# Giving the last two heads of one middle store, and of the last one, to the first four DMA engines

## The chip, the cores and the metric

One core of a Trainium2 chip. The metric is the device time of one execution in microseconds (us). A program on one core is compared by several executions of both kernels on the same chip.

## The reference, cut to what matters

```python
batch, seq, heads, dim = 16, 512, 16, 64
q_rot = rope(q, cos, sin); k_rot = rope(k, cos, sin)       # rotate halves of dim
scores = np.einsum('bshd,bthd->bsht', q_rot, k_rot)        # float32, 16 x 512 x 16 x 512
```

The result has 268 MB, the inputs 67 MB. Four fifths of what moves are stores of scores.

## The kernel before

The work goes in 64 steps (`NST = B * C`). A step makes the scores of 128 rows for all 16 heads: eight pairs of matmuls into PSUM, eight ScalarE copies into a stage tile of 128 x 16 x 512 floats (32 KB a row), one store of 4 MB from SP's queue. There are three stage tiles.

```python
stage_pool = ctx.enter_context(tc.tile_pool(name="stage", bufs=3))
...
def store(i, st):
    o = o_v[i // C, i % C]
    if i < NST - 1:
        nc.sync.dma_start(o, st)          # 128 rows: all 16 engines, 8 rows each
        return
    h = H - 2
    nc.sync.dma_start(o[:, :h], st[:, :h])
    nc.sync.dma_start(o[:116, h:], st[:116, h:])   # 116 rows: 4 engines, 29 rows each
    nc.sync.dma_start(o[116:, h:], st[116:, h:])   # 12 rows: 12 engines, one row each
...
for i in range(C, NST):
    ...                                    # transposes, rope on VectorE, scores(), store(i, st)
    if i % C == C - 2:
        load("q", i // C + 2)              # after steps 6, 10, ... 30, 34, ...
    elif i % C == C - 1:
        load("k", i // C + 3)              # after steps 7, 11, ... 31, 35, ...
```

The last store already hands most of its last two heads to four DMA engines.

## Time and profile before

| | before |
|---|---|
| median of 3 runs | 800.3 us (800.18 to 802.09) |
| profiled span | 799.0 us |
| busiest compute engine | PE, 87% |
| transfers of SP's queue | 98.6% of 16 engines' time |
| mean rate | 421 GB/s |

How to read it: DMA is at its limit, the compute engines are not. But a share of 98.6% over sixteen engines does not tell whether all of them are the limit. For that the packets have to be followed one by one, which the prediction does. It calls the engine that ends last X. The lines themselves are in the prediction.

### The profile page before, as it was taken

The page shows a single profiled execution, that of the slowest core. Times are in us where ns is not written, and L with a number is a line of the kernel's source. Part 1 is how long each engine was busy: PE and PEld are TensorE (multiplying, and loading weights), DVE is VectorE, ACT ScalarE, POOL GpSimd, SP SyncE. Part 2 cuts the span into 40 slices and gives each one's busy share as a digit, 9 for nine tenths or more (in the row PEclk, how much of TensorE's full clock was granted, in tenths as well). Part 3 has the DMA queues.
Part 4 walks back from the last instruction along what each step waited for, and adds up shares of the span by engine and source line. Part 5 has one row for each costly group of instructions (what it writes and reads, how often), then busy time and mean ns, then how long its engine had stood idle before and what let it go on. Part 6 is the DMA issues. An engine that isn't in the chain of part 4 may idle for free.

```text
span 799.0 us, 7715 instructions
## 1 busy us (share of the span) xinstructions
PE 691.3 (87%) x3072; PEld 299.3 (37%) x3072; DVE 544.6 (68%) x516; ACT 561.2 (70%) x647; POOL 0.7 (0%) x6
## 2 busy tenths in 40 slices
PE   4989998997979979799797997979979799799970
PEld 2444443343434334343343443424434343344420
DVE  6999987676866768577585775857758478585300
ACT  3888886775857758577585775757757677578870
POOL 0000000000000000000000000000000000000000
PEclk9999999898998989889898898988989899899995
DMA  9999999999999999999999999999999999998995
GB/s 355 422 424 424 432 427 433 425 435 427 421 437 426 439 427 430 433 431 430 431 428 433 434 428 429 433 438 420 418 426 434 435 415 418 426 440 375 422 439 231
DMA packets 17844, 336.17 MB, mean 421 GB/s; under 512 B 1808, under 2 KB 3088, under 8 KB 4240
## 3 DMA queue, kind: packets, MB, share of 16 engines
q1 hardware_dynamic: 17520, 335.55, 98.6%
q8 instruction: 24, 0.39, 0.2%
q10 hardware_dynamic: 288, 0.13, 0.1%
q14 instruction: 12, 0.10, 0.0%
HBM read 67.24 MB, written 268.44 MB: 420 GB/s over the span
## 4 chain that ended last, share of the span: by engine, by line
DMA 50%; PE 40%; ACT 4%; DVE 3%; issue 1%; ACTq 0%; SPq 0%; DVEq 0%
DMA out_dram<-st 47%; PE ps L166 30%; PE bank L127 10%; ACT st L173 4%; DMA q_sb<-in_q_dram 2%; DVE part L106 1%; DMA early<-in_k_dram 1%; DVE q_sb L107 0%; DVE k_sb L107 0%; DVE k_sb L111 0%; DVE q_sb L111 0%; DVE early L107 0%; DVE kT_t L142 0%; ACTq L281 0%; DVE early L111 0%
## 5 line engine op out<-in xcount | busy, mean ns | idle before, releaser
L173 ACT COPY st<-ps 128x1024 f32<-128x1024 f32 x512 | 494.7, 1018 | 203.7 <-DMA out_dram<-st 105.6
L166 PE MATMUL ps<-kT_t,qT_t 64*128 64x512 f32 x2048 | 548.9, 654 | 71.0 <-ACT st L173 70.9
L166 PEld LDWEIGHTS ps<-kT_t,qT_t 64*128 64x128 f32 x2048 | 185.0, 197 | 261.7 <-issue 144.6
L142 DVE COPY qT_t<-bank 128x512 f32<-128x512 f32 x118 | 81.6, 691 | 203.8 <-PE bank L127 203.8
L127 PEld LDWEIGHTS bank<-ident,q_sb 128*128 128x128 f32 x480 | 55.6, 152 | 102.5 <-issue 99.1
L127 PE MATMUL bank<-ident,q_sb 128*128 128x128 f32 x480 | 86.9, 308 | 0.9 <-PE ps L166 0.9
L127 PEld LDWEIGHTS bank<-ident,k_sb 128*128 128x128 f32 x480 | 50.5, 141 | 95.4 <-issue 38.7
L127 PE MATMUL bank<-ident,k_sb 128*128 128x128 f32 x480 | 78.7, 287 | 1.6 <-DVE qT_t L142 1.2
L142 ACT COPY kT_t<-bank 128x512 f32<-128x512 f32 x122 | 72.5, 599 | 6.4 <-PE bank L127 6.4
L107 DVE TENSOR_TENSOR q_sb<-q_sb,cos_t 128x1024 f32<-128x1024 f32 x60 | 73.5, 1226 | 2.1
L111 DVE TENSOR_TENSOR k_sb<-k_sb,part 128x1024 f32<-128x1024 f32 x60 | 73.5, 1225 | 2.1
L107 DVE TENSOR_TENSOR k_sb<-k_sb,cos_t 128x1024 f32<-128x1024 f32 x60 | 73.5, 1225 | 2.0
L106 DVE TENSOR_TENSOR part<-q_sb,ss_t 128x1024 f32<-128x1024 f32 x60 | 73.5, 1225 | 2.0
L106 DVE TENSOR_TENSOR part<-k_sb,ss_t 128x1024 f32<-128x1024 f32 x60 | 73.0, 1216 | 0.1
L111 DVE TENSOR_TENSOR q_sb<-q_sb,part 128x1024 f32<-128x1024 f32 x60 | 73.0, 1216 | 0.0
L127 PE MATMUL bank<-ident,early 128*128 128x128 f32 x64 | 10.5, 316 | 12.5 <-DVE early L111 10.6
L127 PEld LDWEIGHTS bank<-ident,early 128*128 128x128 f32 x64 | 8.3, 161 | 17.5 <-issue 13.4
L106 DVE TENSOR_TENSOR part<-early,ss_t 128x1024 f32<-128x1024 f32 x8 | 9.8, 1223 | 5.9 <-DMA early<-in_k_dram 5.8
L111 DVE TENSOR_TENSOR early<-early,part 128x512 f32<-128x512 f32 x16 | 10.3, 687 | 0.2
L107 DVE TENSOR_TENSOR early<-early,cos_t 128x1024 f32<-128x1024 f32 x8 | 9.8, 1225 | 0.3
L142 ACT COPY qT_t<-bank 128x512 f32<-128x512 f32 x10 | 5.7, 617 | 3.2 <-PE bank L127 3.2
L142 DVE COPY kT_t<-bank 128x512 f32<-128x512 f32 x6 | 4.1, 685 | 0.3 <-PE bank L127 0.3
(9 smaller groups left out, 2.8 us busy)
## 6 DMA issues: line engine op xcount, KB each, us to landing
out_dram<-st SPq DMA_DIRECT2D x59, 4096.0 KB, 23.9
k_sb<-in_k_dram SPq DMA_DIRECT2D x15, 2048.0 KB, 26.9
q_sb<-in_q_dram SPq DMA_DIRECT2D x15, 2048.0 KB, 29.9
out_dram<-st SPq DMA_DIRECT2D x16, 1024.0 KB, 14.3
out_dram<-st SPq DMA_DIRECT2D x1, 3584.0 KB, 20.4
early<-in_k_dram SPq DMA_DIRECT2D x1, 1536.0 KB, 8.9
early<-in_q_dram SPq DMA_DIRECT2D x1, 1536.0 KB, 12.1
early<-in_k_dram SPq DMA_DIRECT2D x1, 512.0 KB
```

The lines of the kernel that those rows point to most:

```text
L106: nc.vector.tensor_tensor(pv, xs, ss, op=mult)
L107: nc.vector.tensor_tensor(xc, xc, cs, op=mult)
L111: nc.vector.tensor_tensor(y, y, z, op=add)
L127: nc.tensor.transpose(bank[:, x, :], src, ident)
L142: copy(out=dst, in_=src)
L166: nc.tensor.matmul(out=po, lhsT=lhs[64 * r : 64 * r + 64, :], rhs=rh, start=True, stop=True)
L173: nc.scalar.copy(out=so, in_=si)
```

## The change

The intent is to take bytes from the engines that end late and give them to the four lowest-numbered ones, once at step 30 and more completely in the last store. Transfers of 116 and of 4 rows run on engines 0 to 3 only, as the prediction derives.

```diff
+    UNEVEN = (30, NST - 1)
...
-        if i < NST - 1:
+        if i not in UNEVEN:
             nc.sync.dma_start(o, st)
             return
         h = H - 2
         nc.sync.dma_start(o[:, :h], st[:, :h])
-        nc.sync.dma_start(o[:116, h:], st[:116, h:])
-        nc.sync.dma_start(o[116:, h:], st[116:, h:])
+        for rows in (slice(0, 116), slice(116, 120), slice(120, 124), slice(124, P)):
+            nc.sync.dma_start(o[rows, h:], st[rows, h:])
```

## The prediction

> **What bounds the kernel now.** I read the page first, top down. It has one row that is full and none among the engines.
>
> ```profile
> span 799.0 us, 7715 instructions
> PE 691.3 (87%) x3072; PEld 299.3 (37%) x3072; DVE 544.6 (68%) x516; ACT 561.2 (70%) x647; POOL 0.7 (0%) x6
> DMA  9999999999999999999999999999999999998995
> q1 hardware_dynamic: 17520, 335.55, 98.6%
> ```
>
> The four compute engines stop short of 90%. The transfers of SP's queue fill 98.6% of what sixteen DMA engines can give in 799.0 us, at a mean of 421 GB/s. So the transfers are the bound, and the open question is whether all sixteen engines are, or one of them. The second view was busy time by stretch, at the end of the run (columns: stretch in us, its length, the engines, granted clock, DMA share, GB/s):
>
> ```profile
> 750.00:777.00 27.00, 23.71 (x100) 9.45 (x100) 3.83 (x5) 21.38 (x23) 0.00 (x0) 0.94 0.99 426
> 777.00:789.00 12.00, 0.20 (x2) 0.00 (x0) 0.00 (x0) 1.32 (x2) 0.00 (x0) 0.73 0.96 408
> 789.00:795.00 6.00, 0.00 (x0) 0.00 (x0) 0.00 (x0) 0.00 (x0) 0.00 (x0) 0.50 0.30 107
> 795.00:799.00 4.00, 0.00 (x0) 0.00 (x0) 0.00 (x0) 0.00 (x0) 0.00 (x0) 0.50 0.04 15
> ```
>
> Here the reader sees that sixteen engines do not end together. From 789 to 795 a mean share of 0.30 is about five of sixteen; after 795 at most one works. Who is it? The trace keeps a record of every DMA packet (queue, start, duration, bytes), not its engine. But on a busy engine the next packet starts 3 to 4 ns before the last one's recorded end, and each engine must work through the same list (8 packets of 32,768 B for a whole store, then one of 4 B for the semaphore). So I followed the packet that ended last (797.64 us) backwards. The chain goes back to 25 us through 935 packets with one gap over 20 ns (329 ns at 745 us, under an instruction fetch). This one engine, which I call X, never rests. Its 32,768-byte store packets have a median of 1.246 us, against 1.213 us over all engines; its 16,384-byte load packets are not slow (0.61 us). X is late by what its stores lose: in the semaphore landings of each store, the sixteenth comes 1.0 us after the fifteenth at 40 us, 3.3 us after it at 437 us and 6.9 us after it at 797.8 us. X is the bound; the other fifteen have slack.
>
> Does X ever wait for the kernel? Each store was issued between 8.2 and 17.4 us before X took its first packet (from store 4 on), so X always has work queued. The third view, the waits, agrees:
>
> ```profile
> ACT st L173 <- DMA out_dram<-st: 105.6, 28, 6.0
> SPq L147 <- ACT st L173: 657.0, 59, 16.6
> ```
>
> ScalarE waits 105.6 us for a free stage buffer, that is for X's last packet of an old store. The chain of waits is the same told in time: a store's flight, then some 20 us of matmuls, then the next.
>
> ```profile
> 408.91 28.12 DMA out_dram<-st
> 437.04 0.04 ACTq L173
> 437.08 0.04 issue
> 437.12 1.02 ACT st L173
> ```
>
> Only the DMA in this chain is X's time; the matmuls run while X works off its backlog.
>
> **What the Trainium skill says.** "DMA: Bandwidth & Descriptors", section "Why a DMA increments its semaphore by 16 and not by 1": a transfer runs on the largest k up to 16 that divides its slowest dimension on both sides, on the lowest-numbered k engines. Then 128 rows give 16 engines, 116 rows give 4 (29 rows each), 12 rows give 12, 4 rows give 4. The trace agrees in number: SP issues 112 transfers, and there are 1776 four-byte packets = 110 x 16 + 4 + 12. X did exactly one 4,096-byte packet at the end, after its 28,672-byte ones, so X is among engines 4 to 11, not among the first four. The same page, "Latency and other measured facts", calls engines 7 and 15 usually slower than the rest; X could be 7, but no record here gives the number. The same page, "Anatomy of one DMA — SWDGE (gpsimd) path", says that DMA engines do not wait on semaphores, only the issuing sequencer does; X's gapless chain agrees.
>
> **The change, part by part.** The store of step 30 (issued at 381.89 us, on X from 396.87 to 406.88) loses its last two heads, 4 KB of 32 KB in each row; these 128 rows go out in transfers of 116 + 4 + 4 + 4 rows, all on engines 0 to 3.
>
> - X, step 30. Before: eight packets, 1.251 us from one start to the next, plus the semaphore, 10.017 us. After: eight of 28,672 B. At the same rate each takes 0.875 x 1.251 = 1.095 us (an estimate; when compute had ended, the trace shows 1.062 us for that size against 1.213 for 32,768, the same ratio). Saved: 8 x 0.156 = 1.25 us.
> - X, last store. Its one row of the 12-row transfer goes to engines 0 to 3: 0.165 us saved (797.471 to 797.636), directly on the end.
> - Engines 0 to 3, step 30. Instead of eight packets of 1.213 us (9.7 us) they get eight of about 1.06 and 32 of 4,096 B. Those took 0.159 us at the median and 0.200 at the mean in the last store: 8.5 + 32 x 0.2 = 14.9 us, 5.2 us more each. Beside X.
> - Engines 0 to 3, last store. Two rows more than their 30, about 0.3 to 0.4 us each. They ended at 794.06 to 794.79, X at 797.64. With X at 797.64 - 1.25 - 0.17 = 796.2, and the others' start also earlier, as it hangs on stage buffers which X frees, they still end about 2 us before it.
> - SP. Four more issues at step 30, two more at the end. The present ones of this kind took:
>
> ```profile
> 778.35 0.70 SPq L152 DMA_DIRECT2D out_dram<-st  x1
> 779.10 1.19 SPq L153 DMA_DIRECT2D out_dram<-st  x1
> ```
>
> Some 3 to 4.5 us of SP's time (an estimate from these two), which delays the q load issued next. At step 30 that load waits 23.7 us in X's queue before its first packet, so this is hidden.
> - Buffers. A stage tile is free when all of its transfers have landed, now five. On engines 0 to 3 this can be later than on X: relative to X they lose 5.2 + 1.25 = 6.4 us, and the fifteenth landing was about 2.7 us ahead of X near 400 us. In the worst case (one of the four is that fifteenth) step 33 may start filling its tile 3.7 us after X is done instead of at once. X's backlog at the following stores is 11.7 us or more, so even that does not empty X's queue.
>
> Sum: -1.25 - 0.17 = -1.42 us, less up to 0.1 for the crowding described below: -1.4. The time becomes 800.3 - 1.4 = 798.9 us, the profiled span 797.6.
>
> **The rivals.**
> - Nothing is gained at step 30, because the 4 KB rows, though moved by other engines, are still read from X's part of the memory and hold X up by as much. For it: X's rate is near what any engine reaches (27.0 GB/s), and in the last store 4,096-byte packets stretched from 0.159 up to 0.5 us. Against it: in that last store engines 0 to 3 read all 116 rows, X's eight among them, while X wrote its eight 28,672-byte packets. These took 1.062 us five times, otherwise 1.080, 1.146 and 1.189. The two in the time of the crowd lost 0.1 us together; the small packets gave way. This rival would make 800.1 us.
> - The four engines become the bound: their extra 5.2 us holds back the buffer, the next stores come late, X runs dry. For it: ScalarE's waits end with a store's last landing, and only three stage tiles exist. Against it: the backlog of 11.7 us. It would make up to 802 us if X lost what the worst case above costs (3.7 us, less the 1.4 gained).
> - The middle part is absorbed: the kernel waits elsewhere later, so what X saves at 400 us is idle time by 740 us. For it: PE is at 87% and busy 29.38 of the 30 us from 720 to 750. Against it: X has no gap after 25 us but the one fetch, and its backlog at the end is still 8 to 11 us. Only the last store's 0.17 us would remain: 800.1 us.
>
> **Range and chances.** All outcomes lie within 0.4% of 800.3. I put some 75% on the main line (798.9), 20% on the two rivals without gain (800.1) and 5% on a loss. Runs of the kernel before scatter from 800.18 to 802.09, which adds more to the upper end than the lower. Range 798.0 to 800.2. Faster by over 2% would need 16 us, ten times what X sheds; slower by as much needs X starved for the same time. Within 2%: 0.985.
>
> **What would show it right or wrong.** In the packets of X, step 30's store should be eight of about 1.095 us in place of 1.25, with the chain still free of gaps; every later landing of X should be about 1.25 us earlier than before, and the issues of the last stores too. After the last 28,672-byte packet X should have nothing, and the trace should end about 1.4 us earlier, still with X. Rival one shows as step-30 packets on X that stay near 1.25 us; rival two as gaps in X's chain after 420 us, or a later last landing of the store of step 30 that delays the issues after it for good; rival three as a gap in X's chain between 410 and 790 us. The prediction is wrong as a whole if the last packet belongs to an engine of the first four, or if the time does not fall by 0.5 us at least.

## The result, and the profile after

| | before | after |
|---|---|---|
| median of 6 runs | 800.85 us (799.82 to 802.09) | 801.0 us (799.6 to 802.69) |
| ratio after / before | | 1.0001, 95% interval 0.9984 to 1.0017 |
| profiled span | 799.0 us | 799.7 us |

A ratio here is the mean time of one kernel's fast runs over that of the other's of the same rounds, so not quite the ratio of the medians. The time did not move. The prediction of 798.9 us, 1.4 us under before, was wrong, and the measured 801.0 lies outside its range of 798.0 to 800.2.

The page after, its first lines:

```profile
span 799.7 us, 7724 instructions
PE 682.3 (85%) x3072; PEld 295.5 (37%) x3072; DVE 544.6 (68%) x516; ACT 561.3 (70%) x647; POOL 0.7 (0%) x6
DMA  9999999999999999999999999999999999998996
q1 hardware_dynamic: 17664, 335.55, 98.5%
```

The bound is the same. The queue has 144 packets more: at step 30, 128 rows make two packets each instead of one, and four transfers on four engines add 4 x 4 packets of 4 B. The 4 x 4 agree with the rule of the largest divisor that the prediction cites. (In the last store 4 + 12 semaphore packets became 4 x 4, the same sum, which shows nothing.)

The end of the run, busy time by stretch after the change (columns as in the prediction):

```profile
750.00:777.00 27.00, 23.28 (x108) 9.31 (x104) 3.90 (x5) 22.04 (x24) 0.00 (x0) 1.00 1.00 426
777.00:789.00 12.00, 0.00 (x0) 0.00 (x0) 0.00 (x0) 0.52 (x1) 0.00 (x0) 0.63 1.00 430
789.00:795.00 6.00, 0.00 (x0) 0.00 (x0) 0.00 (x0) 0.00 (x0) 0.00 (x0) 0.50 0.35 119
795.00:799.70 4.70, 0.00 (x0) 0.00 (x0) 0.00 (x0) 0.00 (x0) 0.00 (x0) 0.50 0.11 38
```

After 795 us the DMA share is 0.11 where it was 0.04: besides X, some of the four favoured engines are now still at work. Their last packet ended at 797.48 us, X's at 798.26 (797.64 before). So X is still the last, but by 0.8 us only.

The waits and the chain after the change:

```profile
ACT st L174 <- DMA out_dram<-st: 122.7, 40, 6.2
SPq L148 <- ACT st L174: 631.6, 57, 16.6
```

```profile
407.15 30.25 DMA out_dram<-st
437.40 0.02 issue
437.43 0.04 ACTq L174
437.46 0.04 issue
437.50 1.02 ACT st L174
```

ScalarE waits 122.7 us for stage tiles instead of 105.6, yet X's chain of packets has no gap after step 30 but one under an instruction fetch. X was not starved; what the other engines wait for costs nothing.

SP's issues around step 30, first before, then after (start, duration in us, engine, line, operation, count):

```profile
381.89 0.33 SPq L147 DMA_DIRECT2D out_dram<-st  x1
382.32 0.89 SPq L79 DMA_DIRECT2D q_sb<-in_q_dram  x1
```

```profile
382.09 0.33 SPq L152 DMA_DIRECT2D out_dram<-st  x1
383.73 3.42 SPq L154 DMA_DIRECT2D out_dram<-st  x4
387.26 0.89 SPq L80 DMA_DIRECT2D q_sb<-in_q_dram  x1
```

The four pieces took 3.42 us of SP, as estimated, and the q load was issued 5 us later. It still lay 18.5 us in X's queue, so the delay itself was hidden.

Now X's packets at step 30. No view of the profile prints single packets; these were read from the trace file and followed as the prediction describes. Before: eight of 1.25 us, the store and the q load behind it together 14.89 us. After: 1.121, 1.095, 1.086, 1.091, 1.095, 1.114 and 1.105 us, close to the 1.10 that was predicted, and then an eighth of 1.581; the first packet of the q load took 1.406 us instead of 0.611. Store and load together: 14.94 us. X had saved 1.25 us and had lost it again within 3 us of time. That is the finding which the experiments had to explain.

Busy time by stretch for 404 to 408 us, before and then after, points the same way:

```profile
404.00:408.00 4.00, 4.00 (x22) 1.83 (x20) 3.90 (x4) 3.76 (x6) 0.00 (x0) 1.00 0.99 414
```

```profile
404.00:408.00 4.00, 4.00 (x21) 1.79 (x20) 3.67 (x3) 3.74 (x5) 0.00 (x0) 1.00 1.00 364
```

The engines are as busy as before (0.99 and 1.00), but move 364 GB/s in place of 414. They are not idle; their packets take longer. But this stretch alone proves little: later runs that lose the same have 375 to 413 GB/s in it (e1, e3, e13), and e6, which loses nothing, has 387. The reading rests on the packets.

### The profile page after: what moved, and what is told of

Its sections match the earlier page's. It is cut to its first block, busy times and chain, and to the rows that moved or that the text cites. A ratio compares the mean times of both kernels' runs of the same rounds, so it can differ in the third digit from the quotient of the medians.

```text
span 799.7 us, 7724 instructions
## 1 busy us (share of the span) xinstructions
PE 682.3 (85%) x3072; PEld 295.5 (37%) x3072; DVE 544.6 (68%) x516; ACT 561.3 (70%) x647; POOL 0.7 (0%) x6
## 4 chain that ended last, share of the span: by engine, by line
DMA 50%; PE 36%; DVE 5%; ACT 5%; issue 1%; ACTq 0%; DVEq 0%
DMA out_dram<-st 50%; PE ps L167 27%; PE bank L128 9%; ACT st L174 5%; DVE part L107 2%; DVE early L112 1%; DVE k_sb L112 1%; DVE k_sb L108 1%; DVE early L108 1%; DMA early<-in_k_dram 1%; DVE kT_t L143 0%; DVE q_sb L108 0%; DVE q_sb L112 0%; ACTq L282 0%; DVE qT_t L143 0%
## 5 line engine op out<-in xcount | busy, mean ns | idle before, releaser
L174 ACT COPY st<-ps 128x1024 f32<-128x1024 f32 x512 | 494.8, 1019 | 203.3 <-DMA out_dram<-st 122.7
L167 PE MATMUL ps<-kT_t,qT_t 64*128 64x512 f32 x2048 | 540.0, 644 | 79.2 <-ACT st L174 79.2
L167 PEld LDWEIGHTS ps<-kT_t,qT_t 64*128 64x128 f32 x2048 | 181.3, 194 | 265.4 <-issue 134.6
```

The costliest lines, as they stand in the source:

```text
L167: nc.tensor.matmul(out=po, lhsT=lhs[64 * r : 64 * r + 64, :], rhs=rh, start=True, stop=True)
L174: nc.scalar.copy(out=so, in_=si)
```

## The experiments

Two measures are used throughout. "Store plus load" is X's time from the first packet of step 30's store to the end of the q load behind it: 14.89 us before, 13.64 us if the 1.25 us are kept. "Excess" of a load is what its 128 packets of 16 KB take over their undisturbed 0.611 us, in sum over all sixteen engines.

The edits below are abridged; words stand for the lists of slices. My first theory, **A**, was chance: a 16 KB instruction fetch is recorded at 406.3 us, and such fetches ride on the DMA engines. The rival, **B**: what X sheds comes back to it by a cause of the change. Four runs on one chip came first.

### e1: the middle part alone

```diff
-        for rows in (four pieces):
+        for rows in ((slice(0, 116), slice(116, P)) if i == NST - 1 else (four pieces)):
```

> Only the store of step 30 is split; the last store is that of the kernel before. Theory A (the slow DMA engine X really sheds about 1.25 us at step 30; the profile after hid it under an instruction fetch of 1.28 us that fell on X by chance, and the last store cost X 0.4 us more than before instead of 0.17 us less): 1.2 us faster than before on average, ratio 0.9985; in the trace X's packets of step 30 take about 1.10 us in place of 1.25, and X's end is 796.4 us plus 1.3 us for each 16 KB instruction fetch and 0.6 us for each 8 KB one that falls on X. Theory B (what X sheds comes back to it, as slower packets or as a wait): ratio 1.000, X's outliers in the microseconds after step 30 in this run too, without a fetch there.

Measured: 800.1 us against 800.44, ratio 1.0000 (0.9987 to 1.0013). X's step-30 packets were seven of 1.09 to 1.11 us and an eighth of 1.453; store plus load 15.21 us. Theory A's 0.9985 is outside the interval, and the loss is there again.

### e2: steps 20 and 40 in place of 30, last store of before

```diff
-    UNEVEN = (30, NST - 1)
+    UNEVEN = (20, 40, NST - 1)
```

(The last store is that of before here and in all that follow, unless told.)

> Two middle stores split, steps 20 and 40; the last store is that of the kernel before. Theory A: twice 1.25 us, 2.5 us faster, ratio 0.9969. Theory B: ratio 1.000. A third reading, the first four engines become the bound when they are given 128 rows of 4 KB twice (about 4.2 us more each time): the last packets belong to them, after 796 us, and the gain is under 1 us.

Measured: 808.76 us, ratio 1.0084 (1.0055 to 1.0112). The six runs fall into two groups, 803.0 and 803.3, and 807.9 to 810.0; what parts them was not looked for. I had thought of the third reading, but not of its size. The end of the run by stretch:

```profile
789.00:795.00 6.00, 0.00 (x0) 0.00 (x0) 0.00 (x0) 0.00 (x0) 0.00 (x0) 0.50 0.52 216
795.00:799.00 4.00, 0.00 (x0) 0.00 (x0) 0.00 (x0) 0.00 (x0) 0.00 (x0) 0.50 0.24 85
799.00:805.00 6.00, 0.00 (x0) 0.00 (x0) 0.00 (x0) 0.00 (x0) 0.00 (x0) 0.50 0.14 54
```

From 795 to 799 a share of 0.24 is four engines of sixteen. The last packet of all, a small one of one of the first four engines, ended at 804.7 us, X's own share at 796.1. One of the four, followed back, took 13.69 us for step 20 and 14.78 for step 40 in place of 9.69: 9.1 us more in all. That used up their slack and more. So engines 0 to 3 cannot take a second middle split of this size.

### e3: the changed kernel again

No edit.

> The changed kernel once more, unaltered. Theory A: on average some 0.8 us faster than before (1.25 at step 30, less 0.4 in the last store), ratio 0.999, and another draw of the fetches that fall on X: step 30 or the load after it no longer has the 1.28 us in this trace unless a fetch record overlaps it. Theory B: ratio 1.000, and X slowed by about 1.3 us at step 30 and the load behind it again.

Measured: 800.71 us against 800.44, ratio 0.9998 (0.9986 to 1.001). X's eighth packet 1.214 us, the load's first packet 1.116, store plus load 14.33 us. A 16 KB fetch leaves a different mark on the engine it falls on: in e1, at 274 us, on an engine other than X, 0.91 us without any packet and then a packet that took 0.50 us longer. On X at step 30 there is no such hole: the next packet starts 6 ns after the last. In e3 the long packets also began at 405.4 us, two microseconds before the next fetch record (407.4). **Theory A fell**: the loss is in all three traces that have the split at step 30, and it is not a fetch.

### e4: which engine is X?

```diff
+        for rows in pieces of 68, 4, 5, 6, 7, 8, 9, 10 and 11 rows:      # last store only
```

> The kernel before with its last two heads of the last store cut in pieces of 68, 4, 5, 6, 7, 8, 9, 10 and 11 rows, so that by the rule of the largest divisor they run on the lowest 4, 4, 5, 6, 7, 8, 9, 10 and 11 engines, one row on each (17 for the 68). The number of 4096-byte packets that the slow engine X does after its 28672-byte ones tells its number: 7 for engine 4, 6 for 5, 5 for 6, 4 for 7, 3 for 8, 2 for 9, 1 for 10, 0 for 11 and more. I expect 4, engine 7. The time is not the point (the last pieces wait for earlier landings): 798 to 803 us.

Measured: one run, 806.52 us (the last pieces waited for semaphores). I first counted four small packets on X and took it for engine 7. That count was wrong: it crossed a pause of 1.4 us and went on with another engine's packets. In the unbroken stretch right behind X's last 28 KB packet (from 801.32 to 802.13 us) there are five, each with its semaphore packet. They must be those of 5, 6, 7, 8 and 9 rows: those of 10 and 11 rows would run on the idle lower engines at the same time, and between 801.32 and 802.45 us no other engine starts a small packet. Only engine 4 gets all five without being one of the first four. **X is engine 4.** I saw this only after e8.

### e5, e6, e7: what disturbs the load?

In e1, e3 and the changed kernel the q load behind step 30 had an excess of 8.8, 9.5 and 10.2 us; before it had 1.9. So X is not alone: in the changed kernel 23 of that load's 128 packets took over 0.64 us, up to nine of them at the same moment; in the kernel before 9 did, up to four at a time. Several engines are slowed. Theory **C** put this down to engines 0 to 3 being late against the rest; theory **D** to small packets or extra issues next to a load.

e5 sends the last two heads of step 30 in four pieces of 32 rows, on all sixteen engines:

```diff
+        for rows in (slice(0, 32), slice(32, 64), slice(64, 96), slice(96, P)):   # i == 30
```

> Step 30 is split as in the change, but its last two heads go out in four pieces of 32 rows, which run on all 16 engines, two rows each; last store as before. In the three runs with the change's step 30 engine X (number 7) saved about 1.25 us in the store and lost 0.7 to 1.6 us in that store's last packet and the first packets of the q load behind it, and the 128 packets of that q load took 8.8 to 10.2 us more than their undisturbed 611 ns in sum over all engines, against 1.9 in the kernel before. Theory C (the loss comes from putting engines 0 to 3 late against the rest): no excess here, the load's sum under 4 us, X's store plus load 14.9 to 15.1 us as before (the same bytes in smaller packets). Theory D (the loss comes from the five issues or the 4 KB packets in front of the load): the sum again 8 us or more and X's store plus load 15.5 us or more.

Measured: one run, 801.01 us. The excess of the load was 7.9 us and X's store plus load 16.1 us, though no engine was favoured. Theory C had said under 4 and at most 15.1, theory D 8 or more and at least 15.5.

e6 issues the four small transfers after the q load:

```diff
                 load("q", i // C + 2)
+                store_late()          # the four pieces of step 30
```

> Step 30 as in the change, but its four small transfers are issued after the q load instead of before it; last store as before. Theory C: engines 0 to 3 do the q load in their usual place, so X's store plus load take 13.6 to 13.8 us (14.89 before), and the disturbance comes one load later, in the k load after step 31 (sum of excess over 5 us there), if at all; time 0 to 1.2 us under before. Theory D: small packets beside or ahead of loads disturb X wherever they are; X's store plus load stay above 14.3.

Measured: 799.65 us against 800.61, ratio 0.9984 (0.9968 to 1.0000). X's store plus load took 13.65 us: here the whole 1.25 us was kept. The q load's excess was 1.7 us, and that of the next load, k after step 31, was 11.0 (0.0 before); X's own packets of that load were not hit (4.88 us, its usual time). At the end the last packet, at 797.5 us, belonged to one of engines 0 to 3; X had ended at 795.4. Theory D had said above 14.3 for store plus load.

e7 moves the split to step 32, with two whole stores between it and the next load:

```diff
+    UNEVEN = (32, NST - 1)
```

> The same split at step 32 instead of 30: two whole stores lie between it and the next load (the q load after step 34). Last store as before. X's packets of step 32 shrink to about 1.10 us (1.25 us saved). Theory C: engines 0 to 3 are still late two stores later, so the q load after step 34 shows the excess (over 5 us in sum, X over 0.5 us in store plus load), as the load after step 22 did in the run with steps 20 and 40. Theory D: nothing is near the load, so no excess, and X keeps 1.25 us.

Measured: one run, 799.48 us. X's eight packets were 1.07 to 1.11 us, none long. The q load after step 34 had an excess of 10.7 us (0.0 before), X lost 0.39 us in it. Theory D had said no excess.

So C fell by e5, and D by e6 and e7. What the three have in common is narrower: the first load after the pieces has long packets on several engines, and X pays what falls into its own share of that load. I call it **F**. That it comes from the engines' packets being shifted against each other in time is my guess; no run shows it, and e5, which favours no engine, hardly supports it.

### e8: a larger last share for seven engines

```diff
-    h = H - 2;  last pieces of 116 and 12 rows
+    h = H - 6;  last pieces of 119, 7 and 2 rows        # engines 0 to 6
```

> No middle split. In the last store the last six heads (12 KB a row) go out in pieces of 119, 7 and 2 rows, which run on engines 0 to 6 only, so X (number 7) does ten heads of its 8 rows and nothing more: 8 x 0.758 us = 6.1 us in place of 8.87 us. The seven engines were about 7 to 9 us ahead of X at the last store and get 18 to 19 rows of 12 KB (0.45 us each, 8.4 us) in place of their share; they should end within 1 us of X. Expected 2.0 to 2.8 us faster than before, ratio 0.997. If crowding on X's memory side takes the gain back (X's packets over 0.85 us in the last store), ratio 1.000.

Measured: 808.36 us, ratio 1.009 (1.0073 to 1.0107). It rested on my wrong count. Busy time in the last stretch:

```profile
799.00:805.00 6.00, 0.00 (x0) 0.00 (x0) 0.00 (x0) 0.00 (x0) 0.00 (x0) 0.50 0.06 25
```

A share of 0.06 is one engine. It started 18 packets of 12 KB at 797.17 us, when the other six of the seven had ended theirs (793.7 to 796.7), and finished at 805.69. The slow engine is among engines 0 to 6, and I had handed it a large share. This agrees with engine 4. The crowding that the expectation named came as well: the slow engine's own eight packets of 20 KB took 8.0 us in place of 6.1, four of them 0.99 to 1.57 us.

### e9, e11, e12: other places for the split

e9 is e7's kernel, timed; e12 has the split at step 28; e11 has it at step 32 and three heads instead of two in the last store's two pieces.

> The kernel with the middle split at step 32 and the last store of before, timed. Theory F (the split frees X by 1.25 us wherever it stands, the first load after it is disturbed on all engines because their order in time has been shifted, and what X pays depends on how much of its own load falls into that disturbance): at step 30 X paid 0.7 to 1.6 us in three runs, here it paid 0.4 in the one trace there is, so some 0.8 us stay: ratio 0.999, a trace whose load after step 34 has an excess over 5 us in sum over the engines and X's packets there up to 0.6 us longer. If the gain is not real at any place, ratio 1.000 with X paying 1.2 us or more.

> Middle split at step 32, and in the last store three heads instead of two in the two transfers of 116 and 12 rows. X does 13 heads of its rows: 8 x 0.986 + 0.24 = 8.1 us in place of 8.9. Engines 0 to 3 get 30 rows of 6 KB instead of 4 KB, some 2.4 us more; they ended 3 us before X in the trace with step 32, so they should end within 1 us of X. Together 1.2 to 1.8 us faster than before, ratio 0.998. If engines 0 to 3 end after X by more than 1 us, the ratio is 1.000 or more.

> The middle split at step 28, last store of before: a store (29) lies between it and step 30 with its q load. X saves 1.25 us in step 28. Theory F: the q load after step 30 is the disturbed one, sum of excess over 5 us, X pays anything from 0 to 1.6 us there depending on where its load falls; loads after it under 4 us in sum.

Measured: e9 799.12 us, ratio 0.9988 (0.9976 to 1.0001); e11 799.81 us, 0.9987 (0.9973 to 1.0000); e12, one run, 799.52 us. The excess of the first load after the split was 11.1, 18.0 and 12.6 us. In e9 X paid nothing in it (4.876 us), in e12 0.45 us, in e11 1.54 us (store plus load 16.42 in place of 14.87). In e9, as in e6, the last packet was not X's: X ended at 795.4 us, one of engines 0 to 3 at 796.4. Busy time from 450 to 456 us, in the kernel before and then in e9, shows the disturbance at its new place:

```profile
450.00:456.00 6.00, 6.00 (x32) 2.72 (x30) 4.80 (x5) 4.90 (x7) 0.00 (x0) 1.00 1.04 445
```

```profile
450.00:456.00 6.00, 6.00 (x32) 2.71 (x30) 4.26 (x5) 4.91 (x6) 0.00 (x0) 1.00 1.01 388
```

445 GB/s became 388, as 414 had become 364 behind step 30. e11 brought no more than e9, although its X had 0.7 us less to do at the end: X lost more than the whole 1.25 us in the load.

### e10: the last store alone

```diff
+    UNEVEN = (NST - 1,)                    # the change's four pieces, no middle split
```

> Only the last store as in the change (pieces of 116, 4, 4 and 4 rows), no middle split. The prediction had X save 0.17 us by it. In the traces with the four pieces X took 9.23 and 9.01 us for its share of the last store, with the two pieces of before 8.87, 8.88, 8.88 and 9.44. So 8.5 to 9.3 here, and a time within 0.4 us of before: ratio 1.000.

Measured: 800.72 us against 800.4, ratio 1.0003 (0.9991 to 1.0016). X's share of the last store took 8.96 us. With the other traces: four pieces 9.23, 9.01 and 8.96 us; two pieces of two heads 8.65 to 8.89 in eleven traces and 9.44 in one (8.86 in the mean). The four pieces do not save X the predicted 0.17 us. In each of the three traces with four pieces one or two of X's eight packets took 1.24 to 1.52 us in place of 1.06.

### e13, e14: step 30 against step 28, on the same chip

e13 is e1's kernel, e14 is e12's.

> The middle split at step 30 alone, a second time. Theory F: X saves 1.25 us in the store and pays 0.6 to 1.6 us in its end and the q load right behind it: store plus load 14.2 to 15.3 us (14.89 before, 13.64 without a loss); sum of excess of that load 8 to 11 us; time within 0.6 us of before, ratio 0.9995 to 1.0005.

> The split at step 28, timed. Theory F: X keeps 0.6 to 1.2 us, as at step 32 (0.9988): ratio 0.9988, the q load after step 30 with 8 to 13 us of excess, X's part in it 0 to 0.6 us. If place does not matter, same ratio as step 30 on the same chip.

Measured: step 30 800.65 us, ratio 0.9993 (0.9979 to 1.0007); step 28 800.11 us, 0.9989 (0.9976 to 1.0001). At step 30 X's eighth packet took 1.767 us, store plus load 14.73; excess 6.5 us, less than expected. At step 28 the eight packets took 1.07 to 1.11 us, the excess came in the load after step 30 (15.4 us), and X paid some 0.8 us there, more than expected. The two ratios do not differ clearly.

### e15, e16: is it the cutting?

e15 sends step 30 as two transfers of 64 whole rows; e16 as 14 heads and 2 heads, both of 128 rows.

```diff
+    for r in (slice(0, 64), slice(64, P)):          nc.sync.dma_start(o[r], st[r])        # e15, i == 30
+    for x in (slice(0, H - 2), slice(H - 2, H)):    nc.sync.dma_start(o[:, x], st[:, x])  # e16, i == 30
```

> Step 30 goes out as two transfers of 64 whole rows, 4 rows of 32 KB on each of 16 engines; nothing is taken from X and there is no small packet. If small packets disturb the load, its sum of excess stays under 4 us (1.9 before). If any change of the engines' order in time does it, it depends on whether two halves change that order: they hardly do, so under 4 us too; over 8 us would say that the cutting itself or the mapping of rows to engines does it.

> Step 30 goes out as 14 heads and 2 heads of all 128 rows, both on 16 engines: eight packets of 28 KB and eight of 4 KB on each, one extra issue, no engine favoured. If the 4 KB packets are what disturbs the load behind them, its sum of excess is 6 us or more, as with the equal pieces (7.9). If the number of issues or the uneven shares do it, under 4 us.

Measured: e16, one run, 800.35 us, excess 4.8 us: between the two expectations, so inconclusive (X's store plus load 15.19 us). e15, one run, 812.38 us, a surprise of 11 us from one store. Busy time from 397 to 403 us, in the kernel before and then in e15:

```profile
397.00:403.00 6.00, 6.00 (x30) 2.60 (x28) 3.85 (x5) 5.33 (x7) 0.00 (x0) 1.00 0.94 401
```

```profile
397.00:403.00 6.00, 2.23 (x12) 0.72 (x8) 2.38 (x3) 0.00 (x0) 0.00 (x0) 0.87 0.99 280
```

All engines are busy (0.99) and move 280 GB/s instead of 401; PE runs dry (2.23 of 6 us). The run shows the rate, not its cause. The excess of the load behind was 10.2 us, without a small packet anywhere: small packets are not needed for the disturbance. But this cut shifts the engines far more than I had expected, so it does not separate cutting from shifting.

## Why the prediction was wrong, point by point

- **What bounds the kernel: right.** One engine without idle time sets the end, before and after. That it may be engine 7 was wrong: it is engine 4.
- **Step 30, minus 1.25 us on X: right.** Seven of X's eight packets were 1.08 to 1.12 us in all four traces (predicted 1.10); at steps 28 and 32 all were 1.07 to 1.11, but for one of 1.27 in e11.
- **"Sum: -1.25 - 0.17 = -1.42 us, less up to 0.1 for the crowding": this is the step that failed.** It took step 30's 1.25 us as kept to the end ("every later landing of X should be about 1.25 us earlier") and had nothing but 0.1 us to set against it. X's store plus load took 14.94, 15.21, 14.33 and 14.73 us, where 13.64 had been due. The loss is 1.30, 1.57, 0.69 and 1.09, in the mean 1.16 us, not 0.1. I had taken the size from the last store, where no load follows. The loss lies in the last packet of the store and in the load behind it, where packets of several engines are long together. Net of it, the middle split gives X 14.80 against 14.89 us: 0.1 us. The trace before held a sign of it: in the load behind step 51, without any split, X's last packet took 1.03 us in place of 0.61 (at 673 us), and X's store plus load 15.27. The prediction looked at the median alone.
- **The last store, minus 0.17 us: wrong.** The small row did leave X, but its 28 KB packets were held up more: the undisturbed 8 x 1.062 us make 8.5, and the four-piece traces have 9.07 us in the mean, 0.2 more than the 8.87 before. It looks like the crowding of the first rival, but three traces against twelve with two pieces, one of which has 9.44, make that likely and no more. With the middle's 0.1 us this makes about zero, and zero was measured twice (1.0001 and 0.9998).
- **Engines 0 to 3 "still end about 2 us before" X: right in order, wrong in size.** In the trace after they ended 0.8 us before X, and with one split in e6 and e9 they ended 2.1 and 1.1 us after it. On the engine that was followed in e2 a middle split cost 4.0 and 5.1 us, about as estimated (5.2); a second one has no room.
- **SP's issues and the buffers: right.** 3.42 us of issue, hidden; no gap in X's chain.
- **The rivals.** The first, no gain at step 30, was nearest in size (800.1), but its sign, packets of 1.25 us at step 30, did not show. The loss came behind the store. The second, the four engines hold back the buffers and X runs dry, did not come true: X's chain shows no such gap, even in e2. The four engines did end last in e2, e6 and e9, but by their own work. The third asked for a gap in X's chain, and there is none.
- **The range was too narrow for the metric.** It ended at 800.2, under the median of before itself. The medians of before in the later sessions were 800.44, 800.61, 800.4 and 801.11. I looked for the cause in instruction fetches and did not find it: X's traces show only fetches of 8 KB, about 0.6 us each, one after 690 us in every trace and a second near 204 us in e4, e10 and e12. Part of the scatter is there before the change can act: in the fourteen traces whose kernels are alike up to there, X begins step 30 between 396.17 and 397.75 us. So the end of a single trace cannot show an effect of 1 us, and where the scatter comes from stays open.

**What stays open.** That the loss follows the split is shown: the first load behind the pieces of the first split had an excess of 6.5 to 18 us in all twelve traces with the four uneven or four equal pieces, where the same load in the kernel before had 0 to 2.6, and the q load after step 30 had 0.5 to 3.5 in the seven traces with no split ahead of it. Why such a load is slow is not. The split is not the only way to it: the kernel before has loads of 8.5 us (near 77 us), 9.7 (near 563) and 13.0 (near 665), and in e4, without a middle split, X lost 0.83 us at step 30 (store plus load 15.72) at an excess of 3.5. Nor does the first load always take it: after e2's second split most of the long packets came in the second load. Nor is it shown that step 28 or 32 is better than step 30: 0.9989 and 0.9988 against 1.0000 and 0.9993, with overlapping intervals. No version was clearly faster than the kernel before; the best, e6, has 0.9984 with an interval that reaches 1.0000.

## What to carry to other kernels

Where one DMA engine is the bound, taking bytes from it works packet by packet as computed, but look at the transfer that follows before counting the gain: here the load behind the split became slow and took back 1.16 of 1.25 us at step 30, and 0 to 1.5 us at steps 28 and 32. The engines that receive the bytes need their own ledger to the end of the run, since the second gift cost 8 us. And an expected gain of 0.2% needs as many runs of the kernel before as it takes to know its own median to that size, before a range is written.

## What the Trainium skill lacked or had wrong

- "DMA: Bandwidth & Descriptors", section "Latency and other measured facts", calls engines 7 and 15 usually slower, and its guess at the cause holds for transfers issued from GpSimd only. All transfers here were issued from SP and ACT, and the slow engine was number 4 (five small packets counted in e4; e8 agrees), at 1.246 us for 32 KB of a store against 1.213, and 0.61 us for a 16 KB load like the rest. I let the page lead me to 7, past its own limit, and paid with e8.
- The same page, "Rules for kernel authors", says of two transfers to disjoint partition halves that they serialize, so don't bother. The advice held, but this row gives no rate: for a store cut into halves of 64 rows the one run (e15) shows 280 GB/s in place of 401, and 812.38 us in place of 801.11.
- No page gives how long an instruction fetch holds up a DMA engine that carries data: about 1.4 us for 16 KB (at 274 us in e1, on an engine other than X), about 0.6 us for 8 KB on X (at 745 us in the trace before).
- No page has the slow load behind a split store: 6.5 to 18 us of excess over 128 packets, at most 2.6 us in the same load before.
